# A seven-product FFN whose weight-quadrant sums are made by accumulating DMAs instead of VectorE

## The chip, the cores and the metric

The kernel runs on one core of a Trainium2 chip. The metric is the device time of one execution in microseconds (us). A core has a matrix engine (TensorE, PE in the profile, with PEld for its weight loads), VectorE (DVE), ScalarE (ACT), GpSimd (POOL) and SyncE (SP). Each engine works through its own list of instructions in order. SP and POOL also issue transfers (DMAs); sixteen DMA engines, shared by all queues, carry them between HBM and the on-chip memory SBUF.

## The reference, cut to what matters

One encoder layer for two inputs of 512 tokens and 1024 channels, all in float32: a half-step feed-forward network (FFN), a mixer of attention and a recurrent memory, a second half-step FFN, a final norm. What the change touches is the first half of each FFN:

```python
def swiglu(x, w_gate, w_up, w_down):
    return (jax.nn.silu(x @ w_gate) * (x @ w_up)) @ w_down
...
x = x + 0.5 * swiglu(rms_norm(x, ffn1_norm), ffn1_w_gate, ffn1_w_up, ffn1_w_down)
```

`w_gate` and `w_up` are 1024 x 2816. Both inputs go through the same weights.

## The kernel before, in words

**Seven products for eight.** For a block of 128 FFN columns the kernel sees a 2 x 2 matrix product. The left matrix has four quadrants: the gate's and the up weights' columns of the block, each cut into the upper and the lower 512 of the 1024 input channels (g0, g1, u0, u1). The right matrix holds the two normalized inputs, cut in the same way. Instead of eight quadrant products the kernel makes seven, called B11, B21, T2, T1, T3, B22, T4 (Winograd's form of Strassen's scheme). B11 and B21 take g0 and g1 as they are and T4 takes u1. The other four take sums: u0 + u1 (T1), g0 - u0 (T3), u0 + u1 - g0 (T2) and g1 minus that (B22). The right sides are sums too, made once per FFN in `right_sums` and kept in the tiles `xc`.

**Splits.** Every operand is cut into a high and a low float32r part: ScalarE copies the source into the high part (rounding), VectorE subtracts that from the source. `w_pair` does it for weights (L240, L241), `put` for the right sides, `split` (L580, L581) for T4's weights. A product is twelve matmuls of 128x128 by 128x512: four channel slices times three pairs of parts.

**A block.** `gu_rest` (L300) runs a block's products in PSUM banks X (mm), Y (pss) and Z (pst). VectorE and ScalarE empty the banks between the products: L311 subtracts or adds after T2, L315 copies T1's bank, L319 and L321 add T3's and B11's, L324 adds B22's, L326 applies silu, L329 adds T4's, and L330 and L331 multiply gate and up. T4 adds into the bank that L319 has just read, so T4's first matmul waits for L319. The results of two blocks go on to `Sides` (L343, L344), which makes the split right sides of the down projection and stores them to HBM (L345, L346) from a ring of rows.

**Order of blocks.** `Up.rest` (L394) runs over the 22 blocks of an FFN in `ORDER`. Seven blocks had B11 and B21 made early, while the right sides were still being prepared (`begin`), and stored to HBM (`kept`); these "kept" blocks have five products left and alternate with full ones for fourteen blocks. The last eight blocks are all full. While PE works on one block, the left sides of the next are prepared: `gu_left_a` (g0, g1), `gu_left_b` (the four sums and their splits: L263, L265, L266, L269) and `gu_left_c` (u1). The raw weights come through `fetch` on SP's queue (L195), one block further ahead, into four buffers of the tag "wr" (4 KB a partition each); the split parts go into four buffers of the tag "w8".

**What sets the order.** A scheduling layer places the instructions of each engine by priority, which follows the order of the program's text; `shifted` moves some up or down (`SOONER`, `LATER`). Waits between engines and for buffers are semaphores set by that layer. An instruction that waits holds up all that stand behind it on its engine or queue.

**POOL before.** In the up-projection stages POOL has no compute and no DMA. It issues the loads of the mixer's gains (`mix_gains`, L596, called from `rest` at the fourteenth block of the first FFN), some tables, and it computes in the mixer.

Of the kernel before, what the change touches and what calls it, by code (L numbers as in the profile page):

```python
# [16 lines left out]
P = 128  # L17
# [9 lines left out]
def encoder(ctx, tc, I, outs):  # L27
# [91 lines left out]
    def f(ap):  # L119
        return ap.bitcast(F32)  # L120
# [109 lines left out]
    def right_sums(xc, k, x0l, x0u, x1l, x1u):  # L230

        V_.tensor_tensor(x0l, x1l, x0l, op=ALU.subtract)
        V_.tensor_tensor(x1l, x1u, x1l, op=ALU.subtract)
# [25 lines left out]
    def gu_left_b(rg, ru, ring):  # L259
        v = lambda t: t.rearrange("p (k c) -> p k c", c=P)  # L260
        a, b = v(ring("s")), v(ring("s"))
        wb, wc = w8_tile(), w8_tile()
        V_.tensor_tensor(a, half(ru, 0), half(ru, 1), op=ALU.add)  # L263
        w_pair(wb[:, :, 1], a)
        V_.tensor_tensor(b, half(rg, 0), half(ru, 0), op=ALU.subtract)  # L265
        V_.tensor_tensor(a, a, half(rg, 0), op=ALU.subtract)  # L266
        w_pair(wb[:, :, 0], a)
        w_pair(wc[:, :, 0], b)
        V_.tensor_tensor(a, half(rg, 1), a, op=ALU.subtract)  # L269
        w_pair(wc[:, :, 1], a)  # L270
        return {T2_: part(wb, 0), T1: part(wb, 1), T3: part(wc, 0), B22: part(wc, 1)}

    def gu_left_c(ru, ring):
        wd = [ring("wd", F32R).rearrange("p (k c) -> p k c", c=P) for _ in range(2)]
        split(half(ru, 1), *wd)
        return {T4: wd}
# [23 lines left out]
    def gu_rest(W, xc, got, ring, mid):  # L300
# [9 lines left out]
        with shifted(SOONER):  # L310
            V_.tensor_tensor(u2, v1, Y, op=ALU.add)  # L311
# [16 lines left out]
        with shifted(SOONER):  # L328
            V_.tensor_tensor(v1, v1, Y, op=ALU.add)  # L329
# [40 lines left out]
    class Up:  # L370
# [23 lines left out]
        def rest(self, raw, at=None, hook=None):  # L394
# [8 lines left out]
            left = gu_left_b(*raw, ring)  # L403
            left.update(gu_left_c(raw[1], ring))
            raw = self.fetch(ORDER[1])
            got = resume(ORDER[0])
            for i, j in enumerate(ORDER):
                W = left
                nxt = ORDER[i + 1] if i + 1 < NF else None
                if nxt is not None:  # L410
                    left = {} if nxt in self.kept else gu_left_a(raw[0])
                    left.update(gu_left_b(*raw, ring))
                    ru = raw[1]
                    raw = self.fetch(ORDER[i + 2]) if i + 2 < NF else None
                then = []
                h = gu_rest(W, self.xc, got, ring, lambda: then.append(resume(nxt)) if nxt in self.kept else None)
# [981 lines left out]
```

## Time and profile before

| What | Value |
|---|---|
| Time, median of 3 runs | 2130.68 us (2130.02 to 2132.34) |
| Profiled execution | 2131.81 us, of it span 2130.0 us |
| TensorE (PE) busy | 2071.1 us, 97% |
| VectorE (DVE) busy | 1579.5 us, 74% |
| ScalarE (ACT) busy | 968.5 us, 45% |
| GpSimd (POOL) busy | 104.1 us, 5% |
| DMA, SP's queue | 358.84 MB, 50.6% of 16 engines |
| DMA, POOL's queue | 1.27 MB, 0.3% of 16 engines |
| TensorE clock granted, mean | 0.997 |

The first FFN's up-projection blocks fill about 70 to 450 us of the span, the second's about 1515 to 1895 us. The page gives, per engine, the busy time; then groups of instructions by source line with their count, busy time and mean duration; and the idle time ahead of them with what ended it. A chain of waits follows the work that ended last back through what released each step. A DMA's landing time is from its issue to the moment all its data is there.

### The profile page before, as it was taken

The numbers are of one execution on the slowest core, as the hardware profiler recorded it, in microseconds if no ns is written. First come the engines' busy times: TensorE is split into PE (matmuls) and PEld (weight loads), VectorE is DVE, ScalarE is ACT, GpSimd is POOL, SyncE is SP. The second block draws the span as 40 slices with busy tenths as digits, with TensorE's granted clock in tenths as the row PEclk, the third lists the DMA queues.
The fourth block names the chain that finished last, engine by engine and source line by source line (L and its number), as shares of the span: only waits on it lengthen the run. The fifth ranks groups of instructions, "written<-read, shape, count | busy, mean of one in ns | idle before, by whom it ended". The sixth has DMA issues, their size and how long they took to land.

```text
span 2130.0 us, 26826 instructions
## 1 busy us (share of the span) xinstructions
PE 2071.1 (97%) x9472; PEld 1689.2 (79%) x9472; DVE 1579.5 (74%) x2817; ACT 968.5 (45%) x1739; POOL 104.1 (5%) x110
## 2 busy tenths in 40 slices
PE   6999999999999999999999999999999999999997
PEld 5877788888888777878887887788877778888885
DVE  7888887776696796574668755754978887786686
ACT  6534444442225466454435654544644444442223
POOL 1000000001000110100102001010000000000002
PEclk9999999999999999999999999999999999999998
DMA  8465554389765222333352232454464654479753
GB/s 266 150 197 186 182 196 142 131 303 378 281 219 162 78 71 64 95 103 97 117 159 81 60 90 79 129 178 158 154 197 159 197 165 166 142 261 386 284 207 122
DMA packets 294486, 361.81 MB, mean 170 GB/s; under 512 B 17776, under 2 KB 187776, under 8 KB 293328
## 3 DMA queue, kind: packets, MB, share of 16 engines
q1 hardware_dynamic: 293760, 358.84, 50.6%
q0 software_dynamic: 592, 1.27, 0.3%
q8 instruction: 74, 1.21, 0.2%
q14 instruction: 60, 0.49, 0.1%
HBM read 255.15 MB, written 104.89 MB: 169 GB/s over the span
## 4 chain that ended last, share of the span: by engine, by line
PE 74%; DVE 10%; DMA 6%; issue 6%; ACT 4%; POOL 0%; SPq 0%; DVEq 0%; ACTq 0%; POOLq 0%
PE mm L678 14%; PE pss L282 13%; PE pst L282 8%; PE mm L523 8%; PE mm L282 7%; PE pss L523 4%; PE pst L523 4%; PE mm L662 3%; PE pso L523 3%; DMA rbuf<-t 2%; DMA wr<-in_ffn_w_up_dram 2%; PE pso L932 1%; PE mm L1106 1%; PE pso L1062 1%; DVE w L241 1%
## 5 line engine op out<-in xcount | busy, mean ns | idle before, releaser
L678 PE MATMUL mm<-xh,w 128*128 128x512 f32 x896 | 292.0, 395 | 0.0
L282 PE MATMUL pss<-xc,w 128*128 128x512 f32 x1056 | 258.4, 391 | 12.4 <-DVE t L311 12.4
L282 PE MATMUL mm<-xc,w 128*128 128x512 f32 x1056 | 256.0, 391 | 2.5 <-ACT f L291 2.4
L282 PE MATMUL pst<-xc,w 128*128 128x512 f32 x1056 | 255.4, 390 | 0.0
L282 PEld LDWEIGHTS pss<-xc,w 128*128 128x128 f32 x1056 | 196.6, 188 | 60.4 <-DVE t L311 20.0
L282 PEld LDWEIGHTS mm<-xc,w 128*128 128x128 f32 x1056 | 196.8, 188 | 46.8 <-ACT f L291 6.6
L282 PEld LDWEIGHTS pst<-xc,w 128*128 128x128 f32 x1056 | 197.3, 188 | 43.2 <-ACT t L315 2.5
L203 DVE TENSOR_TENSOR w<-wr,w 128x1024 fp32r<-128x1024 f32 (+1 forms) x112 | 135.9, 1215 | 106.0 <-ACT w L202 100.7
L678 PEld LDWEIGHTS mm<-xh,w 128*128 128x128 f32 x896 | 167.6, 188 | 32.1
L523 PE MATMUL mm<-w,rt 128*128 128x512 f32 x792 | 185.6, 390 | 1.1 <-DMA rt<-rbuf 1.1
L678 PE MATMUL mm<-xl,w 128*128 128x512 f32 x448 | 176.7, 394 | 0.0
L523 PEld LDWEIGHTS mm<-w,rt 128*128 128x128 f32 x792 | 148.4, 188 | 32.5 <-DMA rt<-rbuf 1.8
L240 ACT ACTIVATE w<-t 128x512 fp32r<-128x512 f32 x176 | 107.0, 628 | 122.8 <-DVE t L266 42.0
L202 ACT ACTIVATE w<-wr 128x1024 fp32r<-128x1024 f32 (+1 forms) x112 | 114.4, 1028 | 99.4 <-PE mm L678 29.4
L241 DVE TENSOR_TENSOR w<-t,w 128x512 fp32r<-128x512 f32 x176 | 118.0, 689 | 44.5 <-ACT w L240 41.5
L282 PE MATMUL pss<-xc,f 128*128 128x512 f32 x528 | 128.4, 392 | 0.0
L282 PEld LDWEIGHTS pss<-xc,f 128*128 128x128 f32 x528 | 98.2, 188 | 23.6 <-DVE t L319 3.6
L580 ACT ACTIVATE w<-wr 128x512 fp32r<-128x512 f32 x72 | 44.6, 631 | 132.4 <-PE pso L523 64.3
L580 ACT ACTIVATE w<-t 128x512 fp32r<-128x512 f32 x82 | 51.6, 632 | 115.9 <-PE pst L523 47.3
L678 PEld LDWEIGHTS mm<-xl,w 128*128 128x128 f32 x448 | 84.3, 188 | 15.7
L523 PE MATMUL pss<-w,rt 128*128 128x512 f32 x396 | 94.0, 389 | 0.0
L523 PE MATMUL pst<-w,rt 128*128 128x512 f32 x396 | 93.7, 389 | 0.0
(316 smaller groups left out, 3644.4 us busy)
## 6 DMA issues: line engine op xcount, KB each, us to landing
rt<-rbuf SPq DMA_DIRECT2D x154, 512.0 KB, 5.8
wr<-in_w_in_dram SPq DMA_DIRECT2D x72, 512.0 KB, 3.6
wr<-in_ffn_w_gate_dram SPq DMA_DIRECT2D x56, 512.0 KB, 5.3
rbuf<-tab SPq DMA_DIRECT2D x90, 256.0 KB, 3.2
wr<-in_ffn_w_up_dram SPq DMA_DIRECT2D x44, 512.0 KB, 4.2
rbuf<-t SPq DMA_DIRECT2D x88, 256.0 KB, 3.5
rbuf<-f SPq DMA_DIRECT2D x66, 256.0 KB, 3.2
rbuf<-R SPq DMA_DIRECT2D x64, 256.0 KB, 3.5
```

The source lines that it names most:

```text
L202: pin(nc.scalar.activation(hi, raw, AF.Copy))
L203: pin(lo_eng.tensor_tensor(lo, raw, f(hi), op=ALU.subtract))
L240: pin(nc.scalar.activation(t[:, 0], src, AF.Copy))
L241: pin(V_.tensor_tensor(t[:, 1], src, f(t[:, 0]), op=ALU.subtract))
L282: nc.tensor.matmul(p, a[:, k, :], xt[:, b, k, :], start=(first and k == 0 and i == 0), stop=(k == HK_ - 1 and i == 2), skip_group_check=True)
L523: nc.tensor.matmul(p, r[:, b, d * P:(d + 1) * P], u[:, a, :], start=(first and q == 0 and k == 0), stop=(q == len(us) - 1 and k == 2), ski ...
L580: nc.scalar.activation(hi, src, AF.Copy)
L662: nc.tensor.matmul(p[b][:, :N], a[:, k, bs], w_[:, kl, :], start=(k == 0 and i == 0), stop=(k == KD - 1 and i == 2))
L678: nc.tensor.matmul(p, a[:, k, :], b, start=(k == 0 and i == 0), stop=(k == n - 1 and i == 2))
L932: nc.tensor.matmul(po, Vst[:, kv_, hk, :], w, start=(kv_ == 0 and i == 0), stop=(kv_ == 3 and i == 1))
L1062: nc.tensor.matmul(po, vm[:, a, t, hs_], b, start=(t == 0 and n == 0), stop=(t == 3 and n == 2))
L1106: nc.tensor.matmul(p[b], a[:, k, bs], w_[:, k - k0, :], start=(k == 0 and i == 0), stop=(k == KD - 1 and i == 2))
```

## The change

The scheme of signs is altered so that every left side is a plain sum: the seven products are taken for the matrix whose up half is negated. T1 then takes u0 + u1, T3 takes g0 + u0, T2 takes u0 + u1 + g0 and B22 takes u0 + u1 + g0 + g1. The signs move to the right sides (`put_neg` for B22's, one subtraction in `right_sums` reversed) and to the operations that empty the banks.

The sums themselves are no longer made by VectorE. A new class `Left` loads u0, g0 and u1 with SP, and POOL issues DMAs that add a second quadrant, read from HBM, onto a tile in SBUF. Each of the two sums of T1 and T3 takes one such DMA; after their split (`first`) the T1 tile is added to in place for T2, and after T2's split (`second`) again for B22 (`third` splits that, and u1 for T4). `first`, `second` and `third` are called at the start, in the middle and at the end of the block before. The load of the Left after the next is issued after `third`, at the end of the block. The gate's columns are fetched whole (`fetch(j, (0,))`) only for full blocks. A Left takes two "wr" buffers, and the gate of a full block a third.

```diff
     def right_sums(xc, k, x0l, x0u, x1l, x1u):
 
         V_.tensor_tensor(x0l, x1l, x0l, op=ALU.subtract)
-        V_.tensor_tensor(x1l, x1u, x1l, op=ALU.subtract)
+        V_.tensor_tensor(x1l, x1l, x1u, op=ALU.subtract)
...
-    def gu_left_b(rg, ru, ring):
-        v = lambda t: t.rearrange("p (k c) -> p k c", c=P)
-        a, b = v(ring("s")), v(ring("s"))
-        wb, wc = w8_tile(), w8_tile()
-        V_.tensor_tensor(a, half(ru, 0), half(ru, 1), op=ALU.add)
-        w_pair(wb[:, :, 1], a)
-        V_.tensor_tensor(b, half(rg, 0), half(ru, 0), op=ALU.subtract)
-        V_.tensor_tensor(a, a, half(rg, 0), op=ALU.subtract)
-        w_pair(wb[:, :, 0], a)
-        w_pair(wc[:, :, 0], b)
-        V_.tensor_tensor(a, half(rg, 1), a, op=ALU.subtract)
-        w_pair(wc[:, :, 1], a)
-        return {T2_: part(wb, 0), T1: part(wb, 1), T3: part(wc, 0), B22: part(wc, 1)}
-
-    def gu_left_c(ru, ring):
-        wd = [ring("wd", F32R).rearrange("p (k c) -> p k c", c=P) for _ in range(2)]
-        split(half(ru, 1), *wd)
-        return {T4: wd}
+    def put_neg(t, k, src):
+
+        nc.scalar.activation(t[:, 0, k, :], src, AF.Copy, scale=-1.0)
+        V_.scalar_tensor_tensor(t[:, 1, k, :], src, -1.0, f(t[:, 0, k, :]), op0=ALU.mult, op1=ALU.subtract)
+
+    class Left:
+
+
+        def __init__(self, views, j):
+            self.v = [[v[:, i * HK_:(i + 1) * HK_, j * P:(j + 1) * P] for i in range(2)] for v in views]
+            g, u = self.v
+            self.ab = wpool.tile([P, 2, HK_, P], F32, tag="wr", bufs=4, name=nm("wr"))
+            self.a22 = wpool.tile([P, 2, HK_, P], F32, tag="wr", bufs=4, name=nm("wr"))[:, 0]
+            nc.sync.dma_start(self.ab[:, 0], u[0])
+            nc.sync.dma_start(self.ab[:, 1], g[0])
+            nc.sync.dma_start(self.a22, u[1])
+            self.plus(0, u[1])
+            self.plus(1, u[0])
+
+        def plus(self, i, src):
+            G_.dma_start(self.ab[:, i], src, accum_op=ALU.add)
+
+        def first(self):
+            wb, self.wc = w8_tile(), w8_tile()
+            w_pair(wb, self.ab)
+            self.plus(0, self.v[0][0])
+            return {T1: part(wb, 0), T3: part(wb, 1)}
+
+        def second(self):
+            w_pair(self.wc[:, :, 0], self.ab[:, 0])
+            self.plus(0, self.v[0][1])
+            return {T2_: part(self.wc, 0)}
+
+        def third(self, ring):
+            w_pair(self.wc[:, :, 1], self.ab[:, 0])
+            wd = [ring("wd", F32R).rearrange("p (k c) -> p k c", c=P) for _ in range(2)]
+            split(self.a22, *wd)
+            return {B22: part(self.wc, 1), T4: wd}
...
-            V_.tensor_tensor(u2, v1, Y, op=ALU.add)
+            V_.tensor_tensor(u2, v1, Y, op=ALU.subtract)
...
-            V_.tensor_tensor(v5, v5, v1, op=ALU.add)
+            V_.tensor_tensor(v5, v5, v1, op=ALU.subtract)
...
-            V_.tensor_tensor(u2, u2, Z, op=ALU.add)
+            V_.tensor_tensor(u2, u2, Z, op=ALU.subtract)
...
-            V_.tensor_tensor(v1, v1, Y, op=ALU.add)
+            V_.tensor_tensor(v1, Y, v1, op=ALU.subtract)
...
-            left = gu_left_b(*raw, ring)
-            left.update(gu_left_c(raw[1], ring))
-            raw = self.fetch(ORDER[1])
+            def follow(i):
+                if i >= NF:
+                    return None, None
+                j = ORDER[i]
+                return (None if j in self.kept else self.fetch(j, (0,))[0]), Left(self.v, j)
+
+            left = raw.first()
+            left.update(raw.second())
+            left.update(raw.third(ring))
+            rg, raw = follow(1)
             got = resume(ORDER[0])
             for i, j in enumerate(ORDER):
-                W = left
+                W, cur = left, raw
                 nxt = ORDER[i + 1] if i + 1 < NF else None
                 if nxt is not None:
-                    left = {} if nxt in self.kept else gu_left_a(raw[0])
-                    left.update(gu_left_b(*raw, ring))
-                    ru = raw[1]
-                    raw = self.fetch(ORDER[i + 2]) if i + 2 < NF else None
+                    left = gu_left_a(rg) if rg is not None else {}
+                    left.update(cur.first())
                 then = []
-                h = gu_rest(W, self.xc, got, ring, lambda: then.append(resume(nxt)) if nxt in self.kept else None)
+
+                def mid():
+                    if nxt in self.kept:
+                        then.append(resume(nxt))
+                    if nxt is not None:
+                        left.update(cur.second())
+
+                h = gu_rest(W, self.xc, got, ring, mid)
                 got = then[0] if then else None
                 if nxt is not None:
-                    left.update(gu_left_c(ru, ring))
+                    left.update(cur.third(ring))
+                rg, raw = follow(i + 2)
...
-    raw0 += up.fetch(0, (1,))
+    raw0 = Left(up.v, 0)
...
-        put(xc[B22], k, x1u)
+        put_neg(xc[B22], k, x1u)
...
-    raw0 = up.fetch(0)
-    W = [gu_left_a(raw0[0])]
+    W = [up.left(0)]
+    raw0 = Left(up.v, 0)
```

More of the change, by code (lines that the diff above doesn't have):

```diff
@@ L1322, in encoder @@
         W.append(up.left(3 + k))
-        put(xc[B22], k, x1u)
+        put_neg(xc[B22], k, x1u)
         right_sums(xc, k, x0l, x0u, x1l, x1u)
```

## The prediction

> **What bounds the kernel now.** I read the page's busy shares first, then the stretches of the two up-projection stages, then the chain of waits in one of them, then the durations and DMA landings by line.
>
> ```profile
> span 2130.0 us, 26826 instructions
> PE 2071.1 (97%) x9472; PEld 1689.2 (79%) x9472; DVE 1579.5 (74%) x2817; ACT 968.5 (45%) x1739; POOL 104.1 (5%) x110
> ```
>
> TensorE (PE) is busy for 97% of the span. The change touches only the up-projection of the two feed-forward networks (FFN). Each FFN has 22 blocks: fourteen alternate a "kept" block (products B11 and B21 made beforehand, five of seven left) with a full one; the last eight are full. Five pairs kept + full (the first, then their sum), then two pairs full + full, as stretches (us, then busy time of PE, weight load, DVE, ACT, POOL, then clock, DMA share, GB/s):
>
> ```profile
> 116.70:150.50 33.80, 33.23 (x145) 26.81 (x145) 28.12 (x44) 14.48 (x24) 0.00 (x0) 1.00 0.58 189
> ...
> sum 170.00, PE 166.04 PEld 133.99 DVE 140.59 ACT 72.36 POOL 0.00; mean PE 33.21 PEld 26.80 DVE 28.12 ACT 14.47 POOL 0.00
> 318.30:356.50 38.20, 38.20 (x169) 31.47 (x170) 29.47 (x46) 16.64 (x27) 0.00 (x0) 1.00 0.45 152
> 356.50:395.00 38.50, 38.27 (x170) 31.36 (x169) 29.38 (x46) 16.88 (x28) 0.00 (x0) 1.00 0.45 153
> ```
>
> A kept pair takes 170/5 = 34.0 us, a late pair about 38.4. The chain of waits in one kept pair (start, us, what) shows what PE alone would need:
>
> ```profile
> 150.49 7.04 PE pss L282 x29
> 157.53 2.72 PE mm L282 x12
> ...
> 176.63 0.47 issue
> 177.10 1.14 ACT w L240 x2
> ...
> 178.81 0.68 DVE w L241
> 179.50 0.61 DVE t L344
> ...
> 180.12 4.09 DMA rbuf<-t
> ...
> 184.24 0.70 DVE t L311
> ```
>
> PE's own longest wait in these stages (total us, times, longest):
>
> ```profile
> PE pss L282 <- DVE t L311: 12.4, 14, 2.3
> ```
>
> Twelve matmuls (one product) take 2.72 us. A kept pair has 5 + 7 products, 32.6 us; two full blocks have 14, 38.1 us. So PE sets the pace: at most 34.0 - 32.6 = 1.4 us per kept pair and 0.3 per late pair can be won, and those 1.4 us are largely PE's wait for VectorE's first sum of a block (L311), which itself waits for a store to free its ring row.
>
> **The change part by part.** *VectorE sums removed.* Four full-width sums per block go:
>
> ```profile
> L263 DVE TENSOR_TENSOR t<-wr x44: 683/692/694, 32.2 to 1853.7; 128x512 f32<-128x512 f32 x44
> L265 DVE TENSOR_TENSOR t<-wr,wr x44: 681/685/694, 32.9 to 1863.2; 128x512 f32<-128x512 f32 x44
> L266 DVE TENSOR_TENSOR t<-t,wr x44: 683/690/694, 67.9 to 1878.1; 128x512 f32<-128x512 f32 x44
> L269 DVE TENSOR_TENSOR t<-wr,t x44: 681/686/692, 72.3 to 1880.7; 128x512 f32<-128x512 f32 x44
> ```
>
> 44 x (0.692 + 0.685 + 0.690 + 0.686) = 121 us of VectorE time. It has 28.1 of 34.0 us to do in a kept pair and 29.4 of 38.4 in a late one, so this is time of an engine that is not the bound. It is worth no more than the PE gaps: 14 kept pairs x 1.4 = 20 us.
>
> *Sign changes.* The negated B22 side uses one operation of the same width in place of another (8 times), and sums in the product tails swap add for subtract: nothing, the width is the same.
>
> *Loads.* Per block SP issues three loads of 256 KB (up upper half, gate upper half, up lower half), and for a full block the 512 KB of gate beside them. A full block now takes three of the four "wr" buffers, where before it took two, and they are freed only by the block's last split. Loads for the next block therefore start later.
>
> *Accumulating DMAs added.* Four per block, 176 in all, 256 KB in pieces of 512 B, on POOL's queue: A0 and A1 add the up halves to the two sums for T1 and T3; A2 adds the gate's upper half once "first" has split both sums; A3 adds its lower half once "second" has split T2's. "third" then splits B22's. Thus load, A0/A1, first, A2, second, A3, third are strictly in series, and the two middle transfers lie between splits that stand in the in-order queues of ScalarE and VectorE. Two SBUF sums with no latency become two DMA round trips. Their price, L from issue to landing, is the one that decides. No accumulating DMA is in the trace; the nearest are the plain ones that POOL issues, and SP's of the same size:
>
> ```profile
> t<-kept SPq DMA_DIRECT2D x28, 256.0 KB, 2.7
> tab<-in_final_norm_dram POOLq DMA_DIRECT2D x2, 256.0 KB, 7.6
> tab<-in_c_tri_dram POOLq DMA_DIRECT2D x1, 256.0 KB, 6.6
> f<-in_c_rope_dram POOLq DMA_DIRECT2D x1, 256.0 KB, 7.6
> gb<-in_k_norm_dram POOLq DMA_DIRECT2D x1, 32.0 KB, 5.8
> wr<-in_ffn_w_up_dram SPq DMA_DIRECT2D x44, 512.0 KB, 4.2
> 490.05 0.91 POOL L610 DMA_DIRECT2D f<-in_c_rope_dram  x1
> 498.69 0.38 POOL L615 TENSOR_SCALAR gb<-gb 128x64 f32<-128x64 f32 x1 [7.20 <-DMA gb<-in_q_norm_dram]
> ```
>
> POOL's transfers take 5.8 us (a small one) to 7.6 us; the rope load is nearest (256 KB from HBM, pieces of 256 B) and I take L = 7.6. Ends for L: 2.7 (SP's plain transfer, far below) and 10, an estimate: 7.6 plus one more 256 KB transfer at 2.7 for the destination's read. Issue costs POOL 0.9 us each, four per block of 17 to 19 us; POOL does nothing else there (0.00 busy above).
>
> The Trainium skill, "DMA: Bandwidth & Descriptors", Anatomy of one DMA — SWDGE (gpsimd) path, fits about 2.0 us plus bytes / 436 GB/s per such DMA. That is an estimated 2.6 us here, and by it the sum would be that of rival 1 below. The trace does not agree: 256 KB from POOL landed after 6.6 and 7.6 us.
>
> *Splits.* Times for the sum:
>
> ```profile
> L241 DVE TENSOR_TENSOR w<-t,w 128x512 fp32r<-128x512 f32 x72 | 48.3, 689 | 20.2 <-ACT w L240 19.0
> L240 ACT ACTIVATE w<-t 128x512 fp32r<-128x512 f32 x72 | 43.7, 627 | 51.3 <-DVE t L266 19.7 <-PE pst L282 14.9 <-DVE t L269 8.4
> L241 DVE TENSOR_TENSOR w<-wr,w 128x1024 fp32r<-128x1024 f32 x13 | 15.9, 1222 | 2.4 <-ACT w L240 2.4
> 382.25 1.23 DVE L241 TENSOR_TENSOR w<-wr,w 128x1024 fp32r<-128x1024 f32 x1 [0.41 <-ACT w L240]
> 383.40 0.68 DVE L331 TENSOR_TENSOR t<-t,t 128x512 f32<-128x512 f32 x1
> ...
> 386.40 0.69 DVE L357 TENSOR_TENSOR t<-t,t 128x512 f32<-128x512 f32 x1
> 387.00 0.69 DVE L344 TENSOR_TENSOR tab<-t,tab 128x512 fp32r<-128x512 f32 x1
> ```
>
> A half-width split after a landing is 0.63 + 0.69 = 1.32 us (ScalarE, then VectorE); queued VectorE operations follow each other every 0.60 us, full-width ones after 1.15.
>
> *Late pairs.* In the built program VectorE's order for one block is: first, subtraction, sum with Y, second, three to five operations, third, tail and side operations, next first. Since A2 waits for first and A3 for second, the loop is L + 1.32 + L + 1.32 + what stands between third and the end of the next first: five operations and the split (5 x 0.60 + 1.15 = 4.15) after an even block, eleven (6.6 + 1.15 = 7.75) after an odd one. Per pair: 4L + 5.28 + 11.9 = 4L + 17.2. On POOL, A0/A1 of the next Left stand ahead of A2 in every second block and wait for a load that starts only after third: about 2 us in SP's queue behind side stores whose splits come some three VectorE operations later, 4.2 to land and 1.8 to issue both, against the 4.15 to first. The difference is 0 to 4 us; I take half, 2. At L = 7.6: 30.4 + 17.2 + 2 = 49.6 us against 38.4: +11.2, times 8 pairs (4 per FFN) = +90 us.
>
> *Kept pairs.* Here second and third of the kept block stand next to each other on VectorE, ahead of the sum with Y that PE's T4 of the full block waits for. From the sum with Y of the full block to that of the kept one PE has 69 matmuls (15.6 us) + 0.7, VectorE 5.4 + L: PE holds it, 16.3. From there to the next: VectorE needs 1.75 (sum, first) + L + 1.32 + L + 1.32 + 0.6 = 2L + 5.0 = 20.2, PE 63 matmuls, 14.3 + 0.7 = 15.0. So VectorE holds it, waiting for two landings. A3 also stands behind A0/A1 of the next full block: about 1 us. Sum 16.3 + 20.2 + 1 = 37.5 against 34.0: +3.5, times 14 = +49 us.
>
> *Start.* The first block of each FFN has A2 and A3 with no block before it; 32 matmuls (7.3 us) stand between T2 and B22 against L + 1.3 = 8.9. With A0/A1 of the second block ahead of A2 I put 5 us per FFN, +10; 0 to 20 as ends.
>
> *Small loads moved.* The four loads of the mixer's gains, on POOL at the very start before, now stand in its queue between accumulates of the last full blocks, with the scaling that waits for one of them:
>
> ```profile
> 2.87 0.93 POOL L599 DMA_DIRECT2D gain<-in_mix_norm_dram  x1
> ...
> 12.02 0.66 POOL L602 TENSOR_SCALAR hn<-hn 128x4 f32<-128x4 f32 x1 [6.04 <-DMA hn<-in_mlstm_head_norm_dram]
> ```
>
> Four issues at up to 0.93 us stand ahead of one A2 or A3: +3 us, once; the scaling waits beside A2's own landing, so its 6 us cost nothing unless A2 lands sooner.
>
> *DMA engines.* A kept pair moved 34.0 x 189 GB/s = 6.4 MB at a share of 0.58, or 19.7 us of full use. The change adds about 2.1 MB, and 2.1 MB more if the destination's read counts: up to 33 us of 37.5. Tight, not the bound; it can lengthen L, and the upper end covers that.
>
> **Sum:** 90 + 49 + 10 + 3 = +152 us. The profiled execution's own time is 2131.8 us (its span 2130.0 and 1.8 around it; 1.1 above the median 2130.7 of the runs shown), so 2284. Each us of L is worth 14 x 2 + 8 x 4 = 60 us: the sum is 60L - 317 + 13, with 317 = 14 x (34.0 - 22.3) + 8 x (38.4 - 19.2).
>
> **Rivals.** *1, faster:* the accumulates land as fast as SP's 256 KB, L = 2.7. Then 2L + 5.0 = 10.4 and 4L + 17.2 = 28.0 lie below PE's times, the removed sums close the kept gaps, and the time is 2131.8 - 20 = 2112. The place is A2 and A3; the point from which it decides is about L = 5.1, where 60L - 317 + 13 is zero. Against it: no POOL transfer landed in under 5.8 us. For it: VectorE's lighter load.
>
> *2, no slower queue but near break-even:* L = 5.8 as the lone small load, no queueing on POOL and no start cost. Kept pairs 16.3 + 16.6 = 32.9 (-1.1 x 14 = -15), late 40.4 (+2.0 x 8 = +16): 2133. With queueing, start and small loads it is 60 x 5.8 - 317 + 13 = +44, 2176. For it: the 5.8 row was issued alone, as A2 and A3 are.
>
> *3, much slower:* the read of the destination, small pieces and fuller DMA engines make L 10 or more. At 10: 60 x 10 - 317 + 13 = +296, 2428; at 12, 2548. For it: the busy DMA engines. Against it: HBM loads of 512 KB land in 4.2 us in this very stage.
>
> *4, the sums are hidden:* the scheduler leaves so much distance that PE never waits. Against it: second and third of a kept block are adjacent on VectorE with A3 between them, so one landing per pair stands open whatever the rest does. It would read 2112 to 2131.
>
> **How the numbers follow.** Forecast, L between 6 and 10: 0.71; rival 1: 0.05; rival 2: 0.08 (of it 0.03 faster, 0.02 within 0.2%, 0.03 slower); rival 3: 0.14; rival 4: 0.02, faster. About 0.2% is what a measurement of this kernel can tell from no change. Faster 0.05 + 0.03 + 0.02 = 0.10, same 0.02, slower 0.88. The range runs from 2150 (L near 5.8, half the queueing) to 2430 (L = 10) and leaves out both tails.
>
> **What would show it.** Right: POOL-issued transfers landing in 6 to 10 us; ScalarE's line 240 and VectorE's line 241 waiting longest for DMA into wr; PE waiting for the sum with Y; late pairs near 50 us, kept pairs near 37; VectorE busy down by about 121 us; mixer and down-projection stages unchanged in length. Wrong: landings under 5 us and pairs at PE's pace, or landings over 10 us, or SP's loads rather than A2 and A3 ending the waits.

## The result, and the profile after

The changed kernel takes 2361.39 us (median of 4 runs, 2359.52 to 2364.43) against 2130.35 us before (2129.37 to 2132.34): a ratio of 1.1086, with a 95% interval of 1.1073 to 1.1099. That is 231 us slower. The forecast was 2284 us, so the sign held and the time lies inside the range of 2150 to 2430, but the sum was 77 us short.

The page of the changed kernel begins with its span, and then has the busy time of each engine:

```profile
span 2362.7 us, 27325 instructions
PE 2149.3 (91%) x9472; PEld 1734.8 (73%) x9472; DVE 1468.9 (62%) x2597; ACT 959.8 (41%) x1695; POOL 330.4 (14%) x286
```

VectorE (DVE) lost 110.6 us. TensorE (PE) has the same 9472 matmuls, yet is busy for 78.2 us longer. Next come the stretches of the two kinds of pairs, in the first network: five kept pairs and then four late ones, cut at every second instance of VectorE's sum that starts a block's tail. The columns are start and end, length, busy time of PE, weight load, DVE, ACT and POOL, granted clock, DMA share and GB/s. First the kernel before:

```profile
91.40:260.70 169.30, 165.31 (x719) 133.38 (x718) 137.12 (x216) 71.72 (x119) 0.00 (x0) 1.00 0.55 180
294.20:448.10 153.90, 153.67 (x677) 126.37 (x676) 121.39 (x188) 68.32 (x111) 0.00 (x0) 1.00 0.48 162
```

Then the changed kernel:

```profile
94.30:329.10 234.80, 189.14 (x720) 149.60 (x720) 114.30 (x169) 71.06 (x110) 51.78 (x40) 0.86 0.78 177
375.70:566.00 190.30, 166.83 (x687) 134.12 (x686) 99.71 (x145) 65.37 (x102) 42.30 (x35) 0.93 0.76 177
```

A kept pair grew from 33.9 to 47.0 us, and a late pair from 38.5 to 47.6. Of the 65.5 us that five kept pairs lost, 41.7 are new idle time of TensorE (234.8 - 189.1 against 169.3 - 165.3) and 23.8 are matmuls that run longer, at a mean granted clock of 0.86. From the first of these stretches to the end of the last the first network took 115.0 us longer (471.7 against 356.7). The same stretch of the second network (1657.4 to 2123.2 us against 1532.5 to 1892.3) took 106.0 us longer, with kept pairs at 45.6 against 34.5 and late ones at 47.3 against 38.3. The two hold 221 of the 232.7 us by which the span grew.

The longest waits of TensorE in these stages of the changed kernel (total us, times, longest) are for three instructions: VectorE's sums at lines 339 and 331, and ScalarE's eviction at line 311:

```profile
PE pss L302 <- DVE t L339: 72.1, 16, 6.0
PE pss L302 <- DVE t L331: 48.2, 15, 4.9
PE mm L302 <- ACT t L311: 45.4, 13, 5.5
```

Behind the first and the last of them stand the splits, which wait for the gate quadrants (the third accumulating transfer, A2, and the fourth, A3):

```profile
ACT w L240 <- DMA wr<-in_ffn_w_gate_dram: 278.3, 57, 9.8
```

The transfers themselves, from the DMA issues (count, KB each, median us from issue to landing) and from the groups at line 279 (ns to issue one, min/median/max):

```profile
wr<-in_ffn_w_up_dram POOLq DMA_DIRECT2D x88, 256.0 KB, 5.6
wr<-in_ffn_w_gate_dram POOLq DMA_DIRECT2D x88, 256.0 KB, 5.0
rbuf<-t SPq DMA_DIRECT2D x88, 256.0 KB, 5.0
```

```profile
L279 POOL DMA_DIRECT2D wr<-in_ffn_w_gate_dram x88: 1267/1282/2453, 63.6 to 2113.7; - x88
```

The accumulates land after 5.0 to 5.6 us, earlier than the 7.6 forecast, and cost GpSimd 1.28 us each to issue instead of 0.9. Stores of t take 5.0 us. The timeline of one kept pair shows how a landing becomes a stall (start, us, what, and in brackets the wait before it), engine after engine:

```profile
239.35 2.60 POOL L279 DMA_DIRECT2D wr<-in_ffn_w_up_dram  x2 [7.25 <-DVE w L241]
241.42 1.84 POOL L279 DMA_DIRECT2D wr<-in_ffn_w_gate_dram  x1
...
248.05 2.52 ACT L240 ACTIVATE w<-wr 128x512 fp32r<-128x512 f32 x3 [7.42 <-DMA wr<-in_ffn_w_gate_dram]
...
248.71 0.69 DVE L241 TENSOR_TENSOR w<-wr,w 128x512 fp32r<-128x512 f32 x1 [9.88 <-ACT w L240]
249.32 0.68 DVE L339 TENSOR_TENSOR t<-t,pss 128x512 f32<-128x512 f32 x1
...
242.23 2.88 PE L302 MATMUL pst<-xc,w 128*128 128x512 f32 x12
250.05 4.82 PE L302 MATMUL pss<-xc,f 128*128 128x512 f32 x12 [4.94 <-DVE t L339]
```

A3 is issued at 241.42, behind the next block's A0 and A1. The third split starts at 248.05, VectorE has been idle for 9.88 us, and the sum at line 339 comes right behind it. TensorE has waited 4.94 us for that sum, and then takes 4.82 us over a product that otherwise takes 2.88. The other half of the same pair has a second stall:

```profile
265.00 0.63 ACT L363 ACTIVATE tab<-t 128x512 fp32r<-128x512 f32 x1 [4.02 <-DMA rbuf<-tab]
265.66 0.69 DVE L364 TENSOR_TENSOR t<-t,tab 128x512 fp32r<-128x512 f32 x1 [3.85 <-ACT tab L363]
269.09 0.69 DVE L331 TENSOR_TENSOR t<-t,pss 128x512 f32<-128x512 f32 x1 [2.74 <-DMA rbuf<-t]
269.83 5.13 PE L302 MATMUL pss<-xc,w 128*128 128x512 f32 x12 [4.64 <-DVE t L331]
```

Here no accumulate is waited for. ScalarE and VectorE wait for stores to free their rows (4.02 and 2.74 us), TensorE waits 4.64 us for line 331, and its next product runs slowly again. The next sum at line 339, which ends the pair, starts at 275.00.

### The profile page after: what moved, and what is told of

It reads as the page before. It is cut to its first block, busy times and chain, and to the rows that moved or that the text cites. A ratio compares the mean times of both kernels' runs of the same rounds, so it can differ in the third digit from the quotient of the medians.

```text
span 2362.7 us, 27325 instructions
## 1 busy us (share of the span) xinstructions
PE 2149.3 (91%) x9472; PEld 1734.8 (73%) x9472; DVE 1468.9 (62%) x2597; ACT 959.8 (41%) x1695; POOL 330.4 (14%) x286
## 3 DMA queue, kind: packets, MB, share of 16 engines
q0 software_dynamic: 93520, 47.42, 16.2%
## 5 line engine op out<-in xcount | busy, mean ns | idle before, releaser
L241 DVE TENSOR_TENSOR w<-wr,w 128x512 fp32r<-128x512 f32 (+1 forms) x176 | 168.3, 956 | 332.7 <-ACT w L240 332.6
L302 PE MATMUL pss<-xc,w 128*128 128x512 f32 x1056 | 281.4, 416 | 49.4 <-DVE t L331 48.2
L302 PE MATMUL mm<-xc,w 128*128 128x512 f32 x1056 | 278.9, 413 | 49.6 <-ACT t L311 45.4
L302 PEld LDWEIGHTS pss<-xc,w 128*128 128x128 f32 x1056 | 211.5, 203 | 106.2 <-DVE t L331 56.4
L240 ACT ACTIVATE w<-wr 128x512 fp32r<-128x512 f32 (+1 forms) x176 | 144.3, 839 | 334.3 <-DMA wr<-in_ffn_w_gate_dram 278.3
L302 PE MATMUL pss<-xc,f 128*128 128x512 f32 x528 | 158.1, 458 | 72.1 <-DVE t L339 72.1
L279 POOL DMA_DIRECT2D wr<-in_ffn_w_gate_dram x88 | 129.2, 1468 | 537.1 <-DVE w L241 488.9
L302 PEld LDWEIGHTS pss<-xc,f 128*128 128x128 f32 x528 | 116.9, 226 | 107.8 <-DVE t L339 81.4
L279 POOL DMA_DIRECT2D wr<-in_ffn_w_up_dram x88 | 114.9, 1464 | 359.0 <-DMA wr<-in_ffn_w_up_dram 226.3
L613 ACT ACTIVATE w<-t 128x512 fp32r<-128x512 f32 x82 | 51.6, 632 | 118.4 <-PE pst L556 58.6
```

The lines of the kernel that those rows point to most:

```text
L240: pin(nc.scalar.activation(t[:, 0], src, AF.Copy))
L241: pin(V_.tensor_tensor(t[:, 1], src, f(t[:, 0]), op=ALU.subtract))
L279: G_.dma_start(self.ab[:, i], src, accum_op=ALU.add)
L302: nc.tensor.matmul(p, a[:, k, :], xt[:, b, k, :], start=(first and k == 0 and i == 0), stop=(k == HK_ - 1 and i == 2), skip_group_check=True)
L613: nc.scalar.activation(hi, src, AF.Copy)
```

## The experiments

Theories: *chain* (splits wait in order for the landings of A2 and A3), *traffic* (added transfers slow the stores and loads around them), *accumulating* (the adding is what makes a transfer dear), *clock* (the low granted clock after a stall is a loss of its own), *queue* (A3 stands behind the next A0 and A1 on GpSimd).

### Sign changes alone

```diff
-        V_.tensor_tensor(b, half(rg, 0), half(ru, 0), op=ALU.subtract)
+        V_.tensor_tensor(b, half(rg, 0), half(ru, 0), op=ALU.add)
...
-            V_.tensor_tensor(u2, v1, Y, op=ALU.add)
+            V_.tensor_tensor(u2, v1, Y, op=ALU.subtract)
...
-        put(xc[B22], k, x1u)
+        put_neg(xc[B22], k, x1u)
```

> The kernel before with the sign changes alone: the B22 side negated, the tails' sums with add and subtract swapped, the four sums still made by VectorE. All theories that put the loss on the accumulating transfers expect 2130 us, within 5 of the kernel before, with VectorE busy near 1579 us. If the negated side or the subtractions cost something, 2140 or more.

Measured: 2131.36 us, ratio 0.9999 [0.9989, 1.0009]; VectorE 1577.6 us busy. The signs cost nothing.

### A2 and A3 issued, but waited for by no split

```diff
-            self.a22 = wpool.tile([P, 2, HK_, P], F32, tag="wr", bufs=4, name=nm("wr"))[:, 0]
+            self.a22t = wpool.tile([P, 2, HK_, P], F32, tag="wr", bufs=4, name=nm("wr"))
+            self.a22 = self.a22t[:, 0]
...
-            self.plus(0, self.v[0][0])
+            G_.dma_start(self.a22t[:, 1], self.v[0][0])
...
-            self.plus(0, self.v[0][1])
+            G_.dma_start(self.a22t[:, 1], self.v[0][1], accum_op=ALU.add)
```

> The changed kernel with A2 and A3 aimed at the unused half of the buffer of the up quadrant: the same 256 KB from the same addresses, issued by GpSimd at the same places of the program, but no split waits for them. Left out: the gate's addition to the sums for T2 and B22, whose splits take T1's sum. Theory 'chain' (the splits wait in order for two landings, and the halved TensorE clock follows from those stalls): 2110 to 2190 us, mean granted clock back to 0.99, TensorE busy back to about 2071 us. Theory 'traffic' (the added transfers fill the DMA engines and slow stores and row loads): the traffic is unchanged, so 2300 us or more, DMA share in the kept pairs still near 0.78.

Measured: 2199.32 us, ratio 1.0314 [1.029, 1.0338], granted clock 0.983: 162 us below the changed kernel. Of TensorE's three long waits two are gone, and the one for line 331 (332 here) stays:

```profile
PE pss L303 <- DVE t L332: 54.9, 18, 5.7
```

So *chain* stands behind the waits for line 339 and for the eviction, and something else behind the wait for line 331. *Chain* explains up to 162 of the 231 us; the time lies 9 us above the interval that it gave. The 162 also holds three other things, which no run here takes apart. A2 writes plainly into an empty half, so 44 of the 176 transfers are lighter (see the fourth experiment). GpSimd issues at other times: in most blocks A3 waits for A2's landing instead of the second split. And the planner moved some splits in the orders of ScalarE and VectorE.

### A2 and A3 left out

```diff
             w_pair(wb, self.ab)
-            self.plus(0, self.v[0][0])
...
-            self.plus(0, self.v[0][1])
```

> The changed kernel without A2 and A3; left out: the gate's addition to the sums for T2 and B22. 'Chain': the same time as with A2 and A3 aimed beside, within 20 us, since the transfers themselves cost nothing. 'Traffic': half of the added accumulates are gone, so about half of the 231 us loss returns, near 2245 us, and it is clearly faster than the kernel with A2 and A3 aimed beside.

Measured: 2163.89 us, ratio 1.0147 [1.0124, 1.0169]. It is 35 us faster than with A2 and A3 aimed beside, more than the 20 of *chain* and far below the 2245 of *traffic*. Both theories hold a part: transfers that no split waits for cost 35 us. TensorE, VectorE, ScalarE and SyncE have the same order of instructions in both kernels, so this difference is the transfers' own. The stretches (same cuts as above), first the five kept pairs with A2 and A3 beside:

```profile
90.30:288.90 198.60, 175.91 (x721) 141.33 (x720) 114.70 (x169) 70.80 (x110) 46.51 (x40) 0.93 0.84 210
```

Then kept and late pairs without them:

```profile
87.50:276.60 189.10, 173.25 (x722) 138.94 (x721) 114.75 (x169) 70.83 (x110) 25.87 (x20) 0.95 0.73 190
310.00:463.40 153.40, 152.93 (x675) 126.34 (x674) 99.99 (x147) 66.92 (x103) 21.75 (x19) 1.00 0.73 199
```

The late pairs are now at 38.4 us, the pace of the kernel before, with TensorE busy for 152.9 of 153.4 us: A0 and A1 cost nothing there, at the same DMA share (0.73) as in the kept pairs. The kept pairs, which also load the kept rows (ten loads of 256 KB in five pairs), still take 37.8 us.

### Plain writes in place of accumulates

```diff
-            G_.dma_start(self.ab[:, i], src, accum_op=ALU.add)
+            G_.dma_start(self.ab[:, i], src)
```

> The changed kernel with plain writes in place of the accumulating ones: the same instructions in the same order on every engine, the same waits. Left out: the additions, so that each quadrant replaces the sum. If the adding itself (the read of the destination) makes the landing late, issue to landing falls from 5.0-5.6 us to under 4, and the time by about 60 us per us, to 2270 or less. If the price is GpSimd's path with 512 pieces, whether it adds or not, issue to landing stays within 0.5 us of that and the time between 2330 and 2370. If the DMA engines count the destination's read, their share in the kept pairs falls below 0.75.

Measured: 2240.57 us, ratio 1.0507 [1.0482, 1.0532]. With the same instructions in the same order on every engine, 121 of the 231 us go when the transfers don't add. Landing and issue of the plain ones (those of the up weights land after 3.9 us):

```profile
wr<-in_ffn_w_gate_dram POOLq DMA_DIRECT2D x88, 256.0 KB, 3.8
```

```profile
L279 POOL DMA_DIRECT2D wr<-in_ffn_w_gate_dram x88: 747/749/816, 62.7 to 1990.3; - x88
```

The software queue's packets, bytes and share of 16 engines' span, first of the changed kernel:

```profile
q0 software_dynamic: 93520, 47.42, 16.2%
```

Then with plain writes, and the stretch of its five kept pairs:

```profile
q0 software_dynamic: 14672, 47.42, 7.6%
```

```profile
87.90:295.90 208.00, 183.00 (x721) 144.64 (x720) 114.18 (x168) 71.01 (x110) 29.91 (x40) 0.92 0.65 201
```

The kernels with no transfer of this kind have 592 packets on that queue, so 256 KB takes (93520 - 592) / 176 = 528 packets when it accumulates and 80 when it doesn't. Adding more than doubles the time on the DMA engines (16.2% of 2362.7 us against 7.6% of 2238.7), and adds 0.53 us to the issue and 1.2 to 1.7 us to the landing; the DMA share of the kept pairs is 0.65 without it and 0.78 with it. TensorE's waits for line 339 and for the eviction at line 311 fall from 72.1 and 45.4 us to 28.0 and 4.6; the one for line 331 stays (49.2). *Accumulating* is confirmed as about half of the loss. It was not the price of GpSimd's path alone, for which the prediction's rows had given 5.8 to 7.6 us.

### Third split moved behind the tail

```diff
-            w_pair(self.wc[:, :, 1], self.ab[:, 0])
+            w_pair(self.wc[:, :, 1], self.ab[:, 0], tc.keep_in_program_order)
```

> The changed kernel with one move: the split for B22 (after A3's landing) is pinned behind the block's tail, so that on VectorE the order is second split, sum with Y that T4 waits for, tail, first split, then third split. Nothing else is changed. Theory 'neighbours' (the landing of A3 stands in front of the sum with Y in VectorE's order, as the prediction's 2L + 5.0 has it): half 2 of a kept pair loses one landing, 5 us or so, and the halved clock behind it; 14 pairs x 5 = -70, 2290 us or less. Theory 'serial loop' (load, A0 and A1, first, A2, second, A3, third in series are already as long as the pair): within 25 us of 2361, and the wait is only moved, to B22's product or to the next first split.

Measured: 2323.48 us, ratio 1.0909 [1.0893, 1.0926], 38 us below the changed kernel: between the two expectations. TensorE's waits:

```profile
PE pst L302 <- ACT t L335: 52.6, 19, 5.4
...
PE pss L302 <- DVE t L339: 5.6, 2, 3.7
```

The wait for line 339 fell from 72.1 to 5.6 us, as *neighbours* said, and kept pairs to 42.7 us (213.4 / 5). But 52.6 us of new waits for ScalarE's eviction at line 335 took its place. ScalarE, also in order, has A3's landing ahead of that eviction, and then a store that must free a row. In the pair with the longest of these waits it waited 1.91 us for the landing and 3.06 for the store, which ended last:

```profile
187.50 0.63 ACT L363 ACTIVATE tab<-t 128x512 fp32r<-128x512 f32 x1 [3.06 <-DMA rbuf<-tab]
```

Late pairs were no better (194.5 us for four). The planner also changed the order of TensorE's products, so the run is not of one move alone.

### Spare matmuls where TensorE stalls

```diff
+        if warm == 3:
+            spare(W[T1], xc[T1])
         product(Y, W[T3], xc[T3], False)
...
+        if warm == 4:
+            spare(W[B22], xc[B22])
         product(Y, W[T4], xc[T4], False)
```

> The changed kernel with 12 spare matmuls into a free accumulator bank ahead of the product that stalls (T4 of the full blocks, T3 of the kept ones) in the first 14 blocks of each network: 28 x 2.72 = 76 us more of TensorE work, put where it waits. Nothing is left out. Theory 'clock' (the halved clock after a stall is itself a part of the loss): the granted clock returns to 0.98 or more, the real products run at 2.72 to 2.9 us, and the time falls, by 20 to 60 us, although there is more work. Rival (the clock is low only while TensorE has time, so it costs nothing): the time stays within 10 us or rises by up to 76.

Measured: 2417.76 us, ratio 1.1347 [1.1318, 1.1376], 56 us above the changed kernel, mean granted clock 0.965 against 0.953. TensorE was busy 59 us longer with 336 more matmuls, which take 76 us at the full clock, so the real ones ran 17 us faster in all. Its waits moved:

```profile
PE pss L302 <- DVE t L339: 81.6, 15, 7.5
PE mm L302 <- ACT t L319: 55.9, 16, 8.9
PE pss L302 <- DVE t L349: 24.5, 14, 2.4
```

The lines are shifted by 8 and more here: 349 stands for 339 of the changed kernel, 339 for 331, 319 for 311. Half of the spares stand ahead of T4 in the full blocks, and that stall fell from 72.1 to 24.5 us. The other half stand ahead of T3 in the kept blocks, and there the stall grew all the same, from 48.2 to 81.6. The wait for the eviction grew from 45.4 to 55.9. So the three together stayed at 162 us (165.7 before) and the spares came on top. The edit also changed the order that the planner gives TensorE (the next block's first product no longer fills gaps between products). The time rose as the expectation's rival said, and *clock* as I had put it failed; what the low clock costs by itself, this run doesn't settle.

### GpSimd's queue reordered

```diff
+                with tc.issue_after(prev.a3.ins):
                     self.plus(0, u[1])
                     self.plus(1, u[0])
```

> The changed kernel with GpSimd's queue alone reordered: A0 and A1 of the next block behind A3 of the block before, instead of ahead of it (or of A2). TensorE's order is the same instruction by instruction. Theory 'queue' (A3 waits behind A0 and A1, which wait for their load: 241.4 against 239.4 us in the pair read above, and 2 us per late pair): -2 us for each of 14 kept and 8 late pairs, about -44, near 2317 us. Rival (the loop is serial, so A0 and A1 pay back later what A3 wins): within 10 us of 2361.

Measured: 2328.80 us, ratio 1.0929 [1.0912, 1.0945]: 33 us below the changed kernel, three quarters of the 44 expected, with TensorE's order the same (the planner moved a few instructions of VectorE, ScalarE and SyncE). The place of A0 and A1 ahead of A3 was a real cost, in the first network all of it in kept pairs (216.4 us for five, 190.8 for four late ones); in the second the late pairs gained too (184.1 us for four against 189.0). A part is given back at the start: the first of these stretches begins at 102.6 us instead of 94.3, since A0 and A1 of the second block now wait for the first block's A3.

### Both together

The later third split and GpSimd's reordered queue in one kernel.

> The changed kernel with the later third split and GpSimd's reordered queue together (38 and 33 us won by each alone). If the two losses are separate: about 2290 us. If both only shorten the same serial loop of load, A0 and A1, first, A2, second, A3, third, which then sets the pace: 2310 or more, near the better of the two.

Measured: 2337.27 us, ratio 1.0977 [1.0959, 1.0996]: worse than either alone. Late pairs gained (186.2 us for four), kept pairs fell back to 44.0 us. The up quadrants' accumulates now land after 7.5 us instead of 5.6. The first stretch begins at 103.5 us, the start cost of the reordered queue. The losses are not separate, as the second half of the expectation said; that the two edits together do worse than each alone it didn't say, and no run here explains it.

### No accumulating transfer at all

```diff
-            self.plus(0, u[1])
-            self.plus(1, u[0])
...
-            self.plus(0, self.v[0][0])
...
-            self.plus(0, self.v[0][1])
```

> The changed kernel with all four accumulating transfers of each block left out; left out of the computation: the quadrant sums, whose splits take the up upper half and the gate upper half as they were loaded. What is left is the new order of splits, the smaller loads, three buffers per full block and 110 us less on VectorE. Theory 'traffic' (A0 and A1 cost what A2 and A3 cost when nobody waits for them, 35 us, by slower stores and loads): 2125 to 2135 us, DMA share in the kept pairs back under 0.6, stores of t near 3.5 us. Theory 'buffers' (three of four buffers per full block delay the loads): still 2150 or more, with waits for loads into wr. If VectorE's 110 us count for anything by themselves: 2110 to 2120.

Measured: 2111.90 us, ratio 0.9912 [0.9898, 0.9927]: faster than the kernel before by 19 us. So the new loads and buffers cost no more than VectorE's relief (1465.3 us busy) brings, and that relief does count: the time lies in the interval of 2110 to 2120 that the expectation gave for it. The order of instructions on TensorE, VectorE, ScalarE and SyncE is that of the kernel with A0 and A1 alone, so the two show what A0 and A1 did to the kept pairs. The five kept pairs without any accumulate, then TensorE's wait for the first sum of a block (line 327 here) and ScalarE's wait for rows of f (line 359):

```profile
87.70:253.80 166.10, 165.22 (x721) 134.11 (x720) 114.70 (x169) 71.49 (x110) 0.00 (x0) 1.00 0.56 185
```

```profile
PE pss L298 <- DVE t L327: 2.7, 4, 1.4
ACT f L359 <- DMA rbuf<-f: 12.4, 5, 4.2
```

And with A0 and A1 alone (lines 329 and 361):

```profile
PE pss L300 <- DVE t L329: 31.8, 12, 4.9
ACT f L361 <- DMA rbuf<-f: 28.8, 8, 4.6
```

With A0 and A1 the DMA share of the kept pairs is 0.73 instead of 0.56, stores of t land after 4.7 us instead of 3.4, and TensorE waits 31.8 us for the first sum. That sum's own wait for its row hardly grew (33.1 us against 30.6). What grew is ScalarE's wait for all rows of the side operations, 75.3 us at line 361 against 33.2, and VectorE, in order, waits for ScalarE behind it ahead of that sum (30.7 us for the operations of line 362 that write t, against 1.0). The expectation of 2125 to 2135 for *traffic* failed: A0 and A1 cost 52 us (2163.9 - 2111.9), not 35. TensorE's wait for the first sum accounts for 29 of them, and matmuls that run longer for 20 (2085.6 us busy against 2065.6).

### Only A0 and A1 by transfer, the other sums by VectorE

```diff
+            self.rg = rg if rg is not None else fetch_w(views[0][:, :, j * P:(j + 1) * P])
...
-            self.plus(0, self.v[0][0])
+            V_.tensor_tensor(self.ab[:, 0], self.ab[:, 0], half(self.rg, 0), op=ALU.add)
...
-                return (None if j in self.kept else self.fetch(j, (0,))[0]), Left(self.v, j)
+                l = Left(self.v, j)
+                return (None if j in self.kept else l.rg), l
```

> The changed kernel with only A0 and A1 as accumulating transfers; the sums for T2 and B22 are made by VectorE from the gate's columns, which are then loaded whole for the kept blocks too. Nothing is left out. By the ledger so far (2112 with no accumulating transfer, 2164 with A0 and A1 alone, half of VectorE's sums back): 2164 to 2185 us, 120 us of the 231 won back by taking the two landings out of the series. If A0 and A1 in series with the load hold the splits as A2 and A3 did: 2250 or more.

Measured: 2309.34 us, ratio 1.0837 [1.0818, 1.0856]: the ledger's 2164 to 2185 failed, and the other half of the expectation, 2250 or more if A0 and A1 in series with the load hold the splits, was met. Every block of this kernel holds three of the four "wr" buffers. It needs the gate's whole columns until VectorE's last sum, just ahead of the third split, so the next block's loads start only then, and A0 and A1 after them:

```profile
238.67 0.69 DVE L241 TENSOR_TENSOR w<-wr,w 128x512 fp32r<-128x512 f32 x1 [0.70 <-ACT w L240]
...
238.00 0.38 SPq L273 DMA_DIRECT2D wr<-in_ffn_w_up_dram  x1
...
241.73 2.60 POOL L280 DMA_DIRECT2D wr<-in_ffn_w_up_dram  x2 [13.51 <-DMA wr<-in_ffn_w_up_dram]
...
249.12 1.06 ACT L240 ACTIVATE w<-wr 128x1024 fp32r<-128x1024 f32 x1 [9.54 <-DMA wr<-in_ffn_w_up_dram]
```

From the third split to the next first is 10.4 us (238.67 to 249.12), a load and an accumulate in series. A0 and A1 are cheap only where a buffer is free early enough.

### A candidate: the sums on GpSimd

Since a kernel without the sums won 19 us, two versions of the kernel before compute them on GpSimd: all four, and only the first two.

```diff
-        V_.tensor_tensor(a, half(ru, 0), half(ru, 1), op=ALU.add)
+        G_.tensor_tensor(a, half(ru, 0), half(ru, 1), op=ALU.add)
...
-        V_.tensor_tensor(b, half(rg, 0), half(ru, 0), op=ALU.subtract)
+        G_.tensor_tensor(b, half(rg, 0), half(ru, 0), op=ALU.subtract)
```

> The kernel before with its four sums computed by GpSimd instead of VectorE (same operations, no accumulating transfer). A 128x512 sum takes GpSimd about 1.4 us in this trace, 5.6 us per block of 17 to 19, where it is idle. If the 19 us that the kernel without any sum won come from VectorE's relief alone, and the sums only need an engine with time: 2112 to 2122 us, faster than both kernels. Rival (four sums of 1.4 us in a chain make the in-order splits late, or the two engines slow each other): 2135 us or more, with ScalarE's splits waiting for GpSimd or VectorE's operations above 0.69 us.

> As the last, but only the first two sums (up halves; gate upper half less up upper half), which depend on loads alone, go to GpSimd; the two that follow in the chain stay on VectorE, which is relieved of 61 us. Half of the gain, 2118 to 2126 us, if relief is what counts; if the longer chain was what cost time with all four on GpSimd, this one is the faster of the two.

Measured: 2156.00 us, ratio 1.0116 [1.0101, 1.0131], with four sums on GpSimd; 2149.31 us, ratio 1.0083 [1.0068, 1.0098], with two. Both are slower than before. The groups of VectorE between 80 and 470 us show a part of the reason, in the kernel before first, then with four sums on GpSimd (count, busy us, mean ns):

```profile
L331 DVE TENSOR_TENSOR t<-t,t 128x512 f32<-128x512 f32 x22 | 15.1, 685 | 0.0
```

```profile
L331 DVE TENSOR_TENSOR t<-t,t 128x512 f32<-128x512 f32 x21 | 22.7, 1080 | 0.5
```

Two instructions of that kernel that overlap, from its timeline:

```profile
139.59 1.67 DVE L357 TENSOR_TENSOR t<-t,t 128x512 f32<-128x512 f32 x1
...
138.97 1.73 POOL L266 TENSOR_TENSOR t<-t,wr 128x512 f32<-128x512 f32 x1 [4.74 <-DVE w L241]
```

VectorE has 176 instructions fewer and is busy just as long (1579.1 us against 1579.5). With two sums on GpSimd it has 88 fewer and is busy for 1584.1 us; there line 331 keeps its 685 ns, and the half-width splits at line 241 average 839 ns against 689. The two-sum version is the faster by 7 us, which the longer chain of four sums would explain too; how much each costs, the runs don't settle. No version that I ran and that computes the whole result beats the kernel before.

## Why the prediction was right or wrong

A row of versions splits the 231 us: 162 for waiting on A2 and A3 (2361.4 - 2199.3), 35 for their mere traffic (2199.3 - 2163.9), 52 for A0 and A1 (2163.9 - 2111.9), less 19 for the relief of VectorE. As differences of neighbours in a row they add up by construction; in another order the parts could have other sizes. The first holds more than the wait, as said.

- **VectorE's sums, worth up to 20 us.** Right in size: 19 us, and rival 1's number of 2112 us for a kernel that never waits for landings was met at 2111.9. A part of this is luck. The prediction looked for all of it in the gaps of the kept pairs, and twelve of the fourteen gave about 11 us (six of the first network 3.3, six of the second 8.2). Most of the rest was won ahead of them: the second tail of the first network starts at 87.7 us instead of 91.4.
- **Signs at nothing.** Right.
- **Loads that "start later".** Named but not priced. In the changed kernel itself they cost little as far as the runs tell (without accumulates there is no loss). They become a loop as soon as every block holds three buffers.
- **L = 7.6 us.** Wrong: 5.0 to 5.6, below all GpSimd rows that I had (5.8 to 7.6), and between the two signs that I had named (6 to 10 for right, under 5 for wrong). A plain transfer of just this shape on the same queue lands in 3.8 to 3.9 us. The Trainium skill, "DMA: Bandwidth & Descriptors", Anatomy of one DMA — SWDGE (gpsimd) path, whose fit gave an estimated 2.6 us, is too low for these runs as well. The issue was 1.28 us, not 0.9.
- **"60 us for each us of L".** This step failed most. With a measured L of 5.3 the sum's own formula gives 60 x 5.3 - 317 + 13 = +14 us, where 231 were measured. The prediction landed in range by luck: an L that was too high covered loops that were too short.
- **Kept pairs, +3.5 us each.** Measured +13.1 (47.0 against 33.9). The mechanism of half 2 was right: second and third next to each other, two landings, A3 behind A0 and A1. From line 339 at 227.97 (in the trace of the same pair) to 249.32 is 21.35 us, where 20.2 + 1 was forecast. But the size met it in part by errors that cancel: A2 and A3 landed after 5.9 and 6.6 us here instead of 7.6, and A3 was issued 2.6 us after the end of the second split (238.83 to 241.42) instead of 1. Half 1 was forecast at 16.3 us, TensorE-bound; it took 25.7 (249.32 to 275.00). What I left out stands in the second timeline above: stores free their rows later than before, and ScalarE and VectorE wait for them in order. I had quoted the wait of line 311 for a store in the profile of before, and counted it only as a gain.
- **Late pairs, 49.6 us.** Measured 47.6. The number is near but its terms are not: with the measured landings it would be about 40. In one late pair ScalarE's first split waits behind a 4.41 us wait for a store, and TensorE's product waits for an eviction that stands behind the splits:

```profile
424.77 0.63 ACT L363 ACTIVATE f<-t 128x512 fp32r<-128x512 f32 x1 [4.41 <-DMA rbuf<-f]
425.79 1.05 ACT L240 ACTIVATE w<-wr 128x1024 fp32r<-128x1024 f32 x1
...
444.61 4.81 PE L302 MATMUL mm<-xc,w 128*128 128x512 f32 x12 [5.36 <-ACT t L311]
```

- **Start +10, small loads +3.** The second tail of the first network starts 2.9 us later than before (94.3 against 91.4). From the end of its last stretch to the second network's second tail it is 7.0 us more (1091.4 against 1084.4), the mixer with its small loads included. The four small loads couldn't be told apart.
- **DMA engines "tight, not the bound".** Wrong to price this at nothing. A kept pair uses 47.0 x 0.78 = 36.7 us of the engines, above my 33 us. The 35 us of A2 and A3's traffic and the slower stores under A0 and A1 go with a fuller share of the kept pairs (0.73 to 0.84, and 0.56 to 0.73). The share alone doesn't decide, since late pairs at 0.73 lost nothing.
- **TensorE's clock.** Missed entirely: I counted stalls, not what follows them. After waits of 4.64 to 5.36 us a product takes 4.81 to 5.13 us instead of 2.88, and the granted clock of the five kept pairs is 0.86 instead of 1.00. The Trainium skill, "TensorE: Matmul & The Clock Gate", Part 1: The HAM clock gate, says that an idle window of about 3.4 us halves the clock. The trace agrees for these long stalls, but not on the length: one product ran slowly after a wait of 2.09 us, and another at full speed after one of 3.54 us. By these rows a wait of 3.4 us is neither needed nor always enough.

```profile
93.46 4.59 PE L302 MATMUL mm<-xc,w 128*128 128x512 f32 x12 [2.09 <-ACT t L311]
...
1689.22 3.01 PE L302 MATMUL pss<-xc,w 128*128 128x512 f32 x12 [3.54 <-DVE t L331]
```

  In the kept pair shown, two stalls (4.94 and 4.64) and two slow products (1.94 and 2.25 more) make 13.8 us, which is the pair's 13.1 and a little more. How much of the 78 us of longer matmuls would be waiting time otherwise stays open.

## What to carry to other kernels

An accumulating DMA isn't a free adder. Price it from the same transfer in a trace of its own (here 5.0 to 5.6 us to land, 1.28 us to issue and more than twice the engine time of a plain one), and ask what stands in order behind the split that waits for it, on ScalarE as well as VectorE. A kernel whose TensorE is at 97% pays for a new stall, then for slow matmuls behind it (after stalls of 4.6 us and more here, and after one of 2.09), and for added traffic at the stores that free the next rows, even if nothing waits for the traffic itself. When several waits share one loop, take the wait away with the transfer still running, and then the transfer, before believing a formula with one slope.

## What the runs showed of the hardware that was not expected

- An accumulate of 256 KB goes out in 528 packets where a plain write takes 80. It uses about 2.1 us of all 16 DMA engines (16.2% less 0.3% of 2362.7 us, by 176) against 0.9.
- With GpSimd at work on sums of its own, VectorE's 128x512 operations from SBUF go from 0.69 to as much as 1.82 us, and GpSimd's sums from 1.28 to as much as 1.82 (1.67 and 1.73 in the pair shown); sums that read PSUM (line 311) stayed at 0.68 (680 ns mean of 21). The Trainium skill, "SBUF — State Buffer", SBUF: two separate sides, states that a VectorE operation with two SBUF inputs and a GpSimd operation that reads SBUF lock each other out of a shared port. These runs agree in kind: the engine that is offloaded gains nothing.
- Accumulates that GpSimd only issues had no such effect: the 128x512 sums of VectorE kept their 0.69 us in the changed kernel.
